# Seven-product pairs of an MLP: deeper look-ahead for weight loads, and convolutions issued one pair later

## The chip, the cores and the metric

The kernel runs on one core of a Trainium2 chip. The metric is device time in microseconds for one execution. Three runs of the kernel before the change took 1497.08 to 1503.07 us, with a median of 1500.95 us. The lines shown below come from one profiled execution.

The profile's engine names are PE (TensorE, matmul), PEld (TensorE's weight load), DVE (VectorE), ACT (ScalarE), POOL (GpSimd) and SP (SyncE). A "q" behind the name means the engine's queue of DMA issues and waits. L346 is line 346 of the kernel file.

## The reference

The kernel computes one layer of a hybrid backbone for 512 latent tokens and 128 context tokens, in float32. Three mixers run side by side, then comes a gated MLP. The change touches only the MLP:

```python
h2 = rms_norm(x, n2) * (1 + sc2) + sh2
u_val, u_gate = jnp.split(dw_conv(h2 @ w_up, f_conv), 2, axis=-1)
x = x + gt2 * ((jax.nn.silu(u_gate) * u_val) @ w_dn)
```

The model width is 1024 and the MLP's is 2816, so `w_up` is 1024 x 5632 and `w_dn` 2816 x 1024. `dw_conv` is a depthwise convolution of width 3 along the tokens.

## The kernel before, in words

All 640 tokens lie along the free dimension; features lie on the 128 partitions. A float32 product is made of three TensorE products of rounded parts: each operand is split into a high part (`wh`, a ScalarE cast, L149) and a low part (`wl`, a VectorE subtraction, L150).

The width of 2816 gives 22 feature tiles. Tiles 0 to 3 are computed plainly, as a value half (`uv`) and a gate half (`ug`). Tiles 4 to 21 are the 18 "pairs": `up_pair(f)` (L1672) computes value and gate together from seven products in place of eight, with sums of weights and sums of activations (a scheme of the Strassen kind). The tokens are cut into halves L and R of 320 columns. One product is 12 matmuls of 128 x 128 by 320 columns. They accumulate in three places: X and Y, the two banks of one large PSUM tile ("g", of which there are two), and Z in a small one ("s"). In the order of the program:

- product 1 into X and product 2 into Y, with the weights of entry 0;
- product 3 into Z and product 4 into X, entry 1;
- product 5 into Y and product 6 into Z, entry 2;
- product 7 into Y, entry 3.

Between them the partial sums are taken out into the tiles `u1` (value) and `u2` (gate): by ScalarE at L1689 (after product 1) and L1699 (4), and by VectorE at L1692 (2), L1696 (3), L1703 (5), L1706 (6) and L1710 (7). After product 7 come the convolutions of `u1` and `u2` (L1711 to L1713): for each one pass on ScalarE (L487) and four VectorE steps (L489). Then `gated` takes a silu on ScalarE (L1632), a multiplication on VectorE (L1633) and a split of the result (L379 on ScalarE, L380 on VectorE).

The pairs are grouped in blocks of 4, 4, 4, 3 and 3. While a block runs, each pair is followed by two or three products of the down projection of the block before it (`down`, L1718). Such a product is 18 or 24 matmuls into one "g" tile, which two or four VectorE steps empty into the residual tile `xa` (L1722). Since there are only two "g" tiles, pair and down products take turns in them.

Weights follow one plan, a list of entries in the order of use; `W(key)` hands out the next. It also issues the loads of the following two entries (`LOOK_L`) and the splits of the following one (`LOOK_S`). A pair has four entries, "st" 0 to 3, each a raw buffer of 128 x 1024. There are three raw buffers and two each for `wh` and `wl`. Entry 0 is one DMA on SyncE's queue (L248). Entries 1 and 2 have a second one that adds to the first in place, and runs on GpSimd's queue (L250), since it accumulates. The other sums of weights are made by VectorE: L258 (for entry 0, from the raw buffers of entries 0 and 1) and L260 (for entry 2, from those of 0 and 1). The weights of the down products have raw buffers and splits of their own (`rawd`, `whd`, `wld`, two each).

The order of the instructions in each engine's queue is not that of the program. A planner in the framework plays the program forward with costs of its own: an engine takes, among the instructions that are ready, the one with the earliest place in the program. Inside `tc.high_priority()` the place is counted as much earlier. That holds for loads, splits, sums of weights and for the lines that take the partial sums out; the convolutions, the gate and L1722 have plain priority. Once planned, the order in a queue is fixed.

Of the kernel before, what the change touches and what calls it, by code (L numbers as in the profile page):

```python
# [30 lines left out]
NF = DFF // P  # L31
GRP = 256
RAWB, WB = 3, 2
# [25 lines left out]
def hybrid_step(ctx: ExitStack, tc: tile.TileContext, a: dict, o: list):  # L59
# [18 lines left out]
    def gtile():  # L78
        return psg.tile([P, 1024], F32, tag="g", name=nm("g"))
# [7 lines left out]
    def body(ps):  # L87
        return ps[:, OFF:OFF + T]
# [44 lines left out]
    def w_load(pieces, kt, n, down=False):  # L133
        if down:
            raw = mlp["ep"].tile([P, 512], F32, tag="rawd", bufs=2, name=nm("rawd"))
        else:
            raw = ring.tile([P, 1024], F32, tag="raw", bufs=RAWB, name=nm("raw"))
        rv = raw[:, :kt * n].rearrange("p (k n) -> p k n", n=n)
        for src, c0, cn in pieces:
            SY.dma_start(out=rv[:, :, c0:c0 + cn], in_=src.rearrange("(k p) n -> p k n", p=P))  # L140
        return raw

    def w_split(raw, kt, n, down=False):
        if down:
            wh, wl = (mlp["ep"].tile([P, 512], F32R, tag=t, bufs=2, name=nm(t)) for t in ("whd", "wld"))
        else:
            wh, wl = (ring.tile([P, 1024], F32R, tag=t, bufs=WB, name=nm(t)) for t in ("wh", "wl"))
        m = kt * n
        S.copy(wh[:, :m], raw[:, :m])  # L149
        V.tensor_sub(wl[:, :m], raw[:, :m], wh[:, :m].bitcast(F32))  # L150
        vh = wh[:, :m].rearrange("p (k n) -> p k n", n=n)
        vl = wl[:, :m].rearrange("p (k n) -> p k n", n=n)
        return vh, vl

    plan = []
# [74 lines left out]

    pidx = {g[0]: i for i, g in enumerate(plan)}
    loaded, split = {}, {}
    LOOK_L, LOOK_S = 2, 1
    used = [0]


# [3 lines left out]
    def st_load(f, j):  # L240
        raw = st_raw[f, j] = ring.tile([P, 1024], F32, tag="raw", bufs=RAWB, name=nm("raw"))
        lo, hi = (raw[:, c:c + 512].rearrange("p (k n) -> p k n", n=P) for c in (0, 512))

        def part(r, kh):
            c0 = r * DFF + f * P
            return w_up[512 * kh:512 * kh + 512, c0:c0 + P].rearrange("(k p) n -> p k n", p=P)

        SY.dma_start(out=lo, in_=part(*((0, 0), (1, 0), (0, 0), (1, 1))[j]))  # L248
        if j in (1, 2):
            G.dma_start(out=lo, in_=part(1, 2 - j), accum_op=ALU.add)  # L250
        if j == 1:
            SY.dma_start(out=hi, in_=part(0, 1))
        return raw

    def st_sums(f, j):

        if j == 0:
            V.tensor_add(st_raw[f, 0][:, 512:], st_raw[f, 0][:, :512], st_raw[f, 1][:, :512])  # L258
        elif j == 2:
            V.tensor_add(st_raw[f, 2][:, 512:], st_raw[f, 0][:, 512:], st_raw[f, 1][:, 512:])  # L260

    def load_of(j):
        key, pieces, kt, n = plan[j]
        return st_load(*key[1:]) if key[0] == "st" else w_load(pieces, kt, n, key[0] == "wd")

    def split_of(j):
        key, pieces, kt, n = plan[j]
        if key[0] == "st":
            st_sums(*key[1:])
        return w_split(loaded[j], kt, n, key[0] == "wd")  # L270

    def W(key):
        i = pidx[key]
        assert i == used[0], (key, i, used[0])
        used[0] += 1
        with tc.high_priority() if i else nullcontext():
            for j in range(i, min(i + LOOK_L + 1, len(plan))):
                if j not in loaded:
                    loaded[j] = load_of(j)
            for j in range(i, min(i + LOOK_S + 1, len(plan))):  # L280
                if j not in split:
                    split[j] = split_of(j)
        return split[i]


# [47 lines left out]
    fcols = cp.tile([P, 3, 2 * NF], F32, name="fcols")  # L333
# [44 lines left out]
    def split_x(src, hi, lo):  # L378
        S.copy(hi, src)  # L379
        V.tensor_sub(lo, src, hi.bitcast(F32))  # L380
# [62 lines left out]
    n = NROW - R_N2  # L443
# [42 lines left out]
    def conv(y, src, w3):  # L486
        S.activation(out=y, in_=src, func=AF.Copy, scale=w3(1))  # L487
        for o0, o1, i0, t in ((1, TS, 0, 0), (0, TS - 1, 1, 2), (TS + 1, T, TS, 0), (TS, T - 1, TS + 1, 2)):
            V.scalar_tensor_tensor(out=y[:, o0:o1], in0=src[:, i0:i0 + o1 - o0], scalar=w3(t), in1=y[:, o0:o1],  # L489
                                   op0=ALU.mult, op1=ALU.add)  # L490
# [76 lines left out]
    for c in range(NCH):  # L567
# [3 lines left out]
        if c in (3, 4):  # L571
            n = c % 4 + 1
# [758 lines left out]
    for i, (sh, lo_, hi_) in enumerate(((8.0, 0.0, 1e9), (0.0, -1e9, 1e9), (0.0, -1e9, 16.0))):  # L1331

        st, t2 = mf[:, 2, :], mf[:, 3, :]
# [145 lines left out]
    for n, (before, steps, after) in enumerate(fill, -2):  # L1479

        if 1 <= n <= len(seq):
            t, j = seq[n - 1]
# [8 lines left out]
        if 0 <= n < len(seq):  # L1491
            t, j = seq[n]
# [29 lines left out]
    fslots = [ep.tile([P, T], F32, name=f"t{i}") for i in range(7)]  # L1522
# [4 lines left out]
    def rt(n=1):  # L1527
        return [slots.pop(0) for _ in range(n)]

    def ft():  # L1530
        return fslots.pop(0)
# [98 lines left out]
    def gated(f, uv, ug):  # L1630

        S.activation(out=ug, in_=ug, func=AF.Silu)  # L1632
        V.tensor_mul(uv, uv, ug)  # L1633
        ac[f] = rt(2)
        split_x(uv, *(t[:, :T] for t in ac[f]))
# [36 lines left out]
    def up_pair(f):  # L1672

        ps = gtile()
        X, Y, Z = ps[:, :HALF], ps[:, 512:512 + HALF], stile()[:, :HALF]

        def prod(out, w, kh, xx, start, stop):

            for k in range(4):
                for i, (ww, hl_) in enumerate(((w[0], 0), (w[0], 1), (w[1], 0))):  # L1680
                    PE.matmul(out=out, lhsT=ww[:, 4 * kh + k, :], rhs=xx(hl_, k), start=start and k == 0 and i == 0,  # L1681
                              stop=stop and k == 3 and i == 2, skip_group_check=True)

        hH2 = h2H, h2L
        u1, u2 = ft(), ft()
        w = W(("st", f, 0))
        prod(X, w, 0, lambda j, k: hH2[j][:, k, L], True, False)
        with tc.high_priority():
            S.copy(u2[:, L], X)  # L1689
        prod(Y, w, 1, lambda j, k: hs[k, 1][j][:, R], True, False)  # L1690
        with tc.high_priority():
            V.tensor_sub(u1[:, R], u2[:, L], Y)  # L1692
        w = W(("st", f, 1))
        prod(Z, w, 0, lambda j, k: hs[k, 0][j][:, L], True, False)
        with tc.high_priority():
            V.tensor_add(u2[:, R], u2[:, L], Z)  # L1696
        prod(X, w, 1, lambda j, k: hH2[j][:, 4 + k, L], False, True)
        with tc.high_priority():
            S.copy(u1[:, L], X)  # L1699
        w = W(("st", f, 2))  # L1700
        prod(Y, w, 0, lambda j, k: hs[k, 0][j][:, R], False, False)
        with tc.high_priority():
            V.tensor_sub(u2[:, R], Y, u2[:, R])  # L1703
        prod(Z, w, 1, lambda j, k: hH2[j][:, 4 + k, R], False, True)
        with tc.high_priority():
            V.tensor_add(u1[:, R], u1[:, R], Z)  # L1706
        w = W(("st", f, 3))
        prod(Y, w, 0, lambda j, k: hs[k, 1][j][:, L], False, True)
        with tc.high_priority():
            V.tensor_sub(u2[:, L], Y, u2[:, L])  # L1710
        ys = [ft() for _ in range(2)]  # L1711
        for y, u, f2 in zip(ys, (u1, u2), (f, NF + f)):
            conv(y, u, lambda tap, f2=f2: fcols[:, tap, f2:f2 + 1])  # L1713
        fslots.extend((u1, u2))
        gated(f, *ys)
        fslots.extend(ys)

    def down(b, nt):  # L1718
        ps = gtile()
        gemm_b(ps, W(("wd", b, nt)), lambda k: ac[fst[b] + k][0], lambda k: ac[fst[b] + k][1], FBLK[b])  # L1720
        for r, (c0, c1) in enumerate(((0, TS), (TS, T))):
            V.scalar_tensor_tensor(out=x1[nt][:, c0:c1], in0=body(ps)[:, c0:c1], scalar=modc[:, 40 + nt, r:r + 1],  # L1722
                                   in1=x1[nt][:, c0:c1], op0=ALU.mult, op1=ALU.add)
        if nt == 7:
            for k in range(FBLK[b]):
                slots.extend(ac.pop(fst[b] + k))
        if b == NB_F - 1:
            yt_ = ft()
            yt = chunks(yt_)
            tr_chunks(x1[nt], lambda c0, n, v: S.copy(yt[:, c0:c0 + n, :], v))  # L1730
            ns_ = slice(nt * P, (nt + 1) * P)
            SY.dma_start(out=y_s[0, :, ns_].rearrange("(c p) d -> p c d", p=P), in_=yt[:, 0:4, :])
            SY.dma_start(out=y_p[0, :, ns_], in_=yt[:, 4, :])
            fslots.append(yt_)
# [12 lines left out]
    for b in range(1, NB_F):  # L1747
        for i in range(FBLK[b]):
            up_pair(fst[b] + i)
            for nt in downs(b, i):  # L1750
                down(b - 1, nt)
    for nt in range(8):
        down(NB_F - 1, nt)

# [33 lines left out]
```

## Time and profile before

| | us |
|---|---|
| median of three runs | 1500.95 |
| the profiled execution | 1501.03 |
| its span on the core | 1498.4 |
| TensorE busy | 1351.9 |
| VectorE busy | 893.0 |
| ScalarE busy | 581.1 |
| GpSimd busy | 217.5 |
| first product 1 of a pair to the end of the last pair, about | 981 to 1458 |

In a row of the order of time, the first two numbers are the start and the duration in us, then come engine, line, operation, the tile written, the tiles read, and the count; brackets at the end give the idle time before it and what ended that. In a row of waits the numbers are the total in us, how often, and the longest. In a row of the chain of waits they are start and duration. A row over a stretch gives its ends, its length, the busy time of PE, PEld, DVE, ACT and POOL with counts, the granted TensorE clock, the DMA share and GB/s.

### The profile page before, as it was taken

The numbers are of one execution on the slowest core, as the hardware profiler recorded it, in microseconds if no ns is written. First come the engines' busy times: TensorE is split into PE (matmuls) and PEld (weight loads), VectorE is DVE, ScalarE is ACT, GpSimd is POOL, SyncE is SP. The second block draws the span as 40 slices with busy tenths as digits, with TensorE's granted clock in tenths as the row PEclk, the third lists the DMA queues.
The fourth block names the chain that finished last, engine by engine and source line by source line (L and its number), as shares of the span: only waits on it lengthen the run. The fifth ranks groups of instructions, "written<-read, shape, count | busy, mean of one in ns | idle before, by whom it ended". The sixth has DMA issues, their size and how long they took to land.

```text
span 1498.4 us, 27051 instructions
## 1 busy us (share of the span) xinstructions
PE 1351.9 (90%) x10985; PEld 1263.0 (84%) x10985; DVE 893.0 (60%) x1863; ACT 581.1 (39%) x1080; POOL 217.5 (15%) x224
## 2 busy tenths in 40 slices
PE   6998999989798999999999899888888787887888
PEld 4898999989687989999988899878777787877887
DVE  4775876776887533433342545985665756566554
ACT  4552235224855322333332354743333333332233
POOL 1011022021343110121200311000101010010000
PEclk9999999999999999999999999999999999999899
DMA  9423421331111533443454442233434334343223
GB/s 277 135 66 91 107 53 36 78 75 37 29 37 48 101 92 102 120 108 97 128 158 122 126 129 72 50 85 81 91 82 98 92 90 98 81 90 89 65 59 108
DMA packets 228079, 137.97 MB, mean 92 GB/s; under 512 B 22037, under 2 KB 221491, under 8 KB 227955
## 3 DMA queue, kind: packets, MB, share of 16 engines
q1 hardware_dynamic: 208563, 126.48, 31.1%
q0 software_dynamic: 19008, 9.44, 5.2%
q8 instruction: 86, 1.41, 0.4%
q10 hardware_dynamic: 384, 0.33, 0.1%
q14 instruction: 38, 0.31, 0.1%
HBM read 129.67 MB, written 6.55 MB: 91 GB/s over the span
## 4 chain that ended last, share of the span: by engine, by line
PE 45%; DVE 17%; DMA 10%; ACT 4%; issue 4%; POOL 3%; SPq 0%; ACTq 0%; POOLq 0%; DVEq 0%
PE g L346 30%; DMA raw<-in_w_up_dram 9%; PE g L1681 6%; DVE t L489 5%; DVE wl L150 4%; ACT wh L149 1%; DVE wld L150 1%; PE s L394 1%; PE s L594 1%; DVE xa L1722 1%; PE g L367 1%; PE s L1420 1%; PE s L1408 1%; PE m L1370 1%; DMA XT<-Xd 1%
## 5 line engine op out<-in xcount | busy, mean ns | idle before, releaser
L149 ACT CAST wh<-raw 128x1024 fp32r<-128x1024 f32 (+1 forms) x176 | 164.8, 945 | 381.8 <-PE g L346 168.6
L150 DVE TENSOR_TENSOR wl<-raw,wh 128x1024 fp32r<-128x1024 f32 (+1 forms) x176 | 192.8, 1098 | 168.5 <-ACT wh L149 158.9
L346 PE MATMUL g<-hH,wh 128*128 128x320 f32 x768 | 186.1, 321 | 3.0 <-DVE xb L702 1.5
L346 PE MATMUL g<-r,whd 128*128 128x320 f32 x704 | 149.7, 334 | 42.6 <-DVE t L1710 31.7
L346 PE MATMUL g<-hL,wh 128*128 128x320 f32 x768 | 183.7, 317 | 0.6 <-DVE hL L442 0.6
L346 PE MATMUL g<-hH,wl 128*128 128x320 f32 x768 | 182.5, 316 | 0.0
L346 PEld LDWEIGHTS g<-r,whd 128*128 128x128 f32 x704 | 121.8, 207 | 48.8 <-DVE t L1710 36.1
L346 PEld LDWEIGHTS g<-hH,wh 128*128 128x128 f32 x768 | 128.8, 191 | 11.3 <-issue 3.9
L346 PEld LDWEIGHTS g<-hL,wh 128*128 128x128 f32 x768 | 130.2, 190 | 3.4 <-issue 1.8
L346 PEld LDWEIGHTS g<-hH,wl 128*128 128x128 f32 x768 | 131.0, 191 | 2.2 <-issue 1.9
L250 POOL DMA_DIRECT2D raw<-in_w_up_dram x36 | 46.4, 1290 | 461.7 <-DMA raw<-in_w_up_dram 383.3
L1681 PE MATMUL g<-r,wh 128*128 128x320 f32 x432 | 101.3, 321 | 0.1
L367 PE MATMUL g<-wh,hH 128*128 128x256 f32 x320 | 94.4, 295 | 3.4 <-DVE xb L702 3.4
L367 PE MATMUL g<-wl,hH 128*128 128x256 f32 x320 | 94.1, 294 | 0.0
L367 PE MATMUL g<-wh,hL 128*128 128x256 f32 x320 | 93.7, 293 | 0.0
L346 PE MATMUL g<-r,wld 128*128 128x320 f32 x352 | 87.9, 327 | 0.0
L1681 PE MATMUL g<-h2H,wh 128*128 128x320 f32 x144 | 51.3, 356 | 40.4 <-DVE xa L1722 38.9
L489 DVE SCALAR_TENSOR_TENSOR t<-t,fcols,t 128x511 f32<-128x511 f32 (+1 forms) x156 | 78.4, 544 | 1.0 <-ACT t L487 1.0
L1681 PEld LDWEIGHTS g<-r,wh 128*128 128x128 f32 x432 | 72.4, 192 | 6.4 <-DVE t L1703 3.3
L346 PE MATMUL g<-oz,wh 128*128 128x320 f32 x384 | 73.8, 314 | 1.3 <-DVE xb L1281 1.2
L1681 PEld LDWEIGHTS g<-h2H,wh 128*128 128x128 f32 x144 | 29.8, 207 | 45.8 <-issue 42.2
L367 PEld LDWEIGHTS g<-wh,hH 128*128 128x128 f32 x320 | 62.8, 196 | 5.2 <-DVE xb L702 3.6
(592 smaller groups left out, 2974.0 us busy)
## 6 DMA issues: line engine op xcount, KB each, us to landing
raw<-in_w_in_dram SPq DMA_DIRECT2D x64, 512.0 KB
raw<-in_w_up_dram SPq DMA_DIRECT2D x90, 256.0 KB
wada<-in_w_ada_dram SPq DMA_DIRECT2D x32, 512.0 KB
raw<-in_w_up_dram POOLq DMA_DIRECT2D x36, 256.0 KB, 4.8
wat<-in_w_ada_dram SPq DMA_DIRECT2D x16, 512.0 KB
rawd<-in_w_down_dram SPq DMA_DIRECT2D x32, 256.0 KB
raw<-in_w_branch_dram SPq DMA_DIRECT2D x24, 256.0 KB
raw<-in_w_out_dram SPq DMA_DIRECT2D x8, 512.0 KB
```

The costliest lines, as they stand in the source:

```text
L149: S.copy(wh[:, :m], raw[:, :m])
L150: V.tensor_sub(wl[:, :m], raw[:, :m], wh[:, :m].bitcast(F32))
L250: G.dma_start(out=lo, in_=part(1, 2 - j), accum_op=ALU.add)
L346: PE.matmul(out=ps[:, OFF + c0:OFF + c1], lhsT=ww[:, k, :], rhs=xx(k)[:, c0:c1], start=(k == 0 and i == 0), stop=(k == kt - 1 and i == 2))
L367: PE.matmul(out=ps[b][:, o:o + GRP], lhsT=xx[:, 4 * kh + k, cs], rhs=ww[:, k, :], start=(kh == 0 and c % 2 == 0 and k == 0 and i == 0), st ...
L394: PE.matmul(out=pa[32 * g:32 * g + 32, :w], lhsT=csil[:, k, :], rhs=t[g], start=start, stop=stop)
L489: V.scalar_tensor_tensor(out=y[:, o0:o1], in0=src[:, i0:i0 + o1 - o0], scalar=w3(t), in1=y[:, o0:o1], op0=ALU.mult, op1=ALU.add)
L594: PE.transpose(pt[:, i * P:(i + 1) * P], src[:, (c0 + i) * P:(c0 + i + 1) * P], ident)
L1370: PE.matmul(out=ps[:, 0:256], lhsT=qT_[t][b, qs], rhs=kT_[t][b, :TS].rearrange("p (r k) -> p r k", k=64)[:, :, CST[j]:CST[j] + 32], start= ...
L1408: PE.transpose(pt[:, i * P:(i + 1) * P], Pt[:, i * P:(i + 1) * P], ident)
L1420: PE.matmul(out=po[64 * e:64 * e + 64, 0:P], lhsT=v[:, h * HD:(h + 1) * HD], rhs=PT[:, i * P:(i + 1) * P], start=(i == 0), stop=(i == len( ...
L1681: PE.matmul(out=out, lhsT=ww[:, 4 * kh + k, :], rhs=xx(hl_, k), start=start and k == 0 and i == 0, stop=stop and k == 3 and i == 2, skip_g ...
```

## The change

Two things are changed. First, in the entries "uv", "ug", "st" and "wd", `W` also issues loads up to six entries ahead (`LOOK_F`), as far as `may_load` allows: the last user of the buffer must have been issued already. Second, `up_pair` no longer issues the convolutions and the gate of its own pair at its end. It puts them into a list `later` as a generator with three parts (convolution of `u2`, convolution of `u1`, gate). `some()` runs one part, and is called at four places in the next pair: after products 4 and 5, and twice after product 6. What is left after the last pair runs behind its down products. The convolution of `u2` now comes ahead of that of `u1`.

```diff
-    LOOK_L, LOOK_S = 2, 1
+    LOOK_L, LOOK_S, LOOK_F = 2, 1, 6
...
+    def may_load(j):
+
+        down = plan[j][0][0] == "wd"
+        same = [i for i in range(j) if (plan[i][0][0] == "wd") == down]
+        n = 2 if down else RAWB
+        if len(same) < n:
+            return down
+        i = same[-n]
+        if i not in split:
+            return False
+        key = plan[i][0]
+        return key[0] != "st" or key[2] > 1 or pidx["st", key[1], 2] in split
...
+            if key[0] in ("uv", "ug", "st", "wd"):
+                for j in range(i + LOOK_L + 1, min(i + LOOK_F + 1, len(plan))):
+                    if j not in loaded:
+                        if not may_load(j):
+                            break
+                        loaded[j] = load_of(j)
...
             S.copy(u1[:, L], X)
+        some()
         w = W(("st", f, 2))
         prod(Y, w, 0, lambda j, k: hs[k, 0][j][:, R], False, False)
         with tc.high_priority():
             V.tensor_sub(u2[:, R], Y, u2[:, R])
+        some()
         prod(Z, w, 1, lambda j, k: hH2[j][:, 4 + k, R], False, True)
         with tc.high_priority():
             V.tensor_add(u1[:, R], u1[:, R], Z)
+        some()
+        some()
         w = W(("st", f, 3))
...
-        ys = [ft() for _ in range(2)]
-        for y, u, f2 in zip(ys, (u1, u2), (f, NF + f)):
-            conv(y, u, lambda tap, f2=f2: fcols[:, tap, f2:f2 + 1])
-        fslots.extend((u1, u2))
-        gated(f, *ys)
+        later.append(finish(f, u1, u2))
+
+    def finish(f, u1, u2):
+
+        ys = []
+        for u, f2 in ((u2, NF + f), (u1, f)):
+            ys.append(ft())
+            conv(ys[-1], u, lambda tap, f2=f2: fcols[:, tap, f2:f2 + 1])
+            fslots.append(u)
+            yield
+        gated(f, ys[1], ys[0])
         fslots.extend(ys)
+        yield
+
+    later = []
+
+    def some():
+        if later:
+            if next(later[0], 0) == 0:
+                later.pop(0)
...
             for nt in downs(b, i):
                 down(b - 1, nt)
+    while later:
+        some()
     for nt in range(8):
         down(NB_F - 1, nt)
```

## The prediction

> **What bounds the kernel now.** I read the busy shares first, then the stage of the pairs alone, then who waited there, then the chain of waits, and last the instructions of one pair in order of time. Engine shares, and the queue of the accumulating loads:
>
> ```profile
> PE 1351.9 (90%) x10985; PEld 1263.0 (84%) x10985; DVE 893.0 (60%) x1863; ACT 581.1 (39%) x1080; POOL 217.5 (15%) x224
> ...
> raw<-in_w_up_dram POOLq DMA_DIRECT2D x36, 256.0 KB, 4.8
> ```
>
> The 90% are an average. The change touches the 18 pairs. Their stretch (columns: us, then PE, PEld, DVE, ACT, POOL busy), the copies of product 1, and one pair in the middle:
>
> ```profile
> 981.20:1458.00 476.80, 396.04 (x2377) 374.82 (x2378) 291.44 (x490) 153.83 (x218) 43.66 (x34) 0.94 0.38 85
> ```
> ```profile
> L1689 ACT COPY t<-g x18: 425/426/429, 983.3 to 1447.7; 128x320 f32<-128x320 f32 x18
> ```
> ```profile
> 1237.41:1264.26 26.85, 22.10 (x132) 20.93 (x132) 16.17 (x28) 8.60 (x12) 2.56 (x2) 0.94 0.40 88
> ```
>
> So TensorE idles 80.8 us in this stage, the turns are (1447.7 - 983.3)/17 = 27.3 us long on average, and the middle one lasts 26.85 us with TensorE busy for 22.10 and VectorE for 16.17. Neither fills it: it must be a loop of latencies. What TensorE waited for between 981 and 1458 us (us in total, times, longest):
>
> ```profile
> PE g L1681 <- DVE xa L1722: 38.9, 14, 3.2
> PE g L346 <- DVE t L1710: 31.7, 17, 2.7
> PE g L346 <- DVE xa L1722: 8.9, 3, 3.2
> ```
>
> Both waits are for VectorE to empty a PSUM tile. The chain of waits gives the loads between two pairs:
>
> ```profile
> 1254.49 1.24 DVE wl L150
> 1255.74 3.15 DMA raw<-in_w_up_dram
> 1259.46 4.77 DMA raw<-in_w_up_dram
> ```
>
> The low part of entry 2 (its "wl") frees a raw buffer, the next pair's entry 1 is loaded into it, GpSimd's accumulating load adds to it, and VectorE's sum L258 takes it at 1259.46 + 4.77 = 1264.23. VectorE from one L258 to the next wl of entry 2:
>
> ```profile
> 1237.41 0.69 DVE L258 TENSOR_TENSOR raw<-raw,raw 128x512 f32<-128x512 f32 x1 [3.92 <-DMA raw<-in_w_up_dram]
> 1238.03 0.48 DVE L1710 TENSOR_TENSOR t<-g,t 128x320 f32<-128x320 f32 x1
> 1238.42 0.68 DVE L260 TENSOR_TENSOR raw<-raw,raw 128x512 f32<-128x512 f32 x1
> 1239.02 0.74 DVE L489 SCALAR_TENSOR_TENSOR t<-t,fcols,t 128x511 f32<-128x511 f32 x1
> 1239.68 1.22 DVE L150 TENSOR_TENSOR wl<-raw,wh 128x1024 fp32r<-128x1024 f32 x1
> 1240.82 0.69 DVE L150 TENSOR_TENSOR wld<-rawd,whd 128x512 fp32r<-128x512 f32 x1
> 1241.43 1.22 DVE L150 TENSOR_TENSOR wl<-raw,wh 128x1024 fp32r<-128x1024 f32 x1
> 1242.56 1.66 DVE L489 SCALAR_TENSOR_TENSOR t<-t,fcols,t 128x511 f32<-128x511 f32 x3
> 1244.15 0.68 DVE L150 TENSOR_TENSOR wld<-rawd,whd 128x512 fp32r<-128x512 f32 x1
> 1244.75 1.26 DVE L489 SCALAR_TENSOR_TENSOR t<-t,fcols,t 128x127 f32<-128x127 f32 x3
> 1245.93 0.74 DVE L1722 SCALAR_TENSOR_TENSOR xa<-g,modc,xa 128x512 f32<-128x512 f32 x1
> 1246.60 0.34 DVE L489 SCALAR_TENSOR_TENSOR t<-t,fcols,t 128x127 f32<-128x127 f32 x1
> 1246.85 1.00 DVE L1722 SCALAR_TENSOR_TENSOR xa<-g,modc,xa 128x128 f32<-128x128 f32 x2
> 1247.80 0.83 DVE L1633 TENSOR_TENSOR t<-t,t 128x640 f32<-128x640 f32 x1
> 1248.54 0.35 DVE L1722 SCALAR_TENSOR_TENSOR xa<-g,modc,xa 128x128 f32<-128x128 f32 x1
> 1249.42 0.82 DVE L380 TENSOR_TENSOR r<-t,r 128x640 fp32r<-128x640 f32 x1 [0.53 <-ACT r L379]
> 1250.61 0.49 DVE L1696 TENSOR_TENSOR t<-t,s 128x320 f32<-128x320 f32 x1 [0.37 <-ACT t L1689]
> 1253.56 0.49 DVE L1692 TENSOR_TENSOR t<-t,g 128x320 f32<-128x320 f32 x1 [2.46 <-PE g L1681]
> 1254.49 1.23 DVE L150 TENSOR_TENSOR wl<-raw,wh 128x1024 fp32r<-128x1024 f32 x1 [0.44 <-ACT wh L149]
> ```
>
> This is the loop. VectorE waits 3.92 us for the load, then works 13 us without a pause, and the tile that the next pair needs ("xa", from the first down product) is emptied only behind seven of the eight convolution steps. TensorE meanwhile:
>
> ```profile
> 1238.56 0.86 PE L346 MATMUL g<-r,whd 128*128 128x320 f32 x4 [1.74 <-DVE t L1710]
> ...
> 1242.20 0.46 PE L1681 MATMUL s<-r,wh 128*128 128x320 f32 x2
> ...
> 1247.34 0.39 PE L1681 MATMUL g<-h2H,wh 128*128 128x320 f32 x1 [2.91 <-DVE xa L1722]
> ...
> 1248.58 0.47 PE L1681 MATMUL g<-h2L,wh 128*128 128x320 f32 x1
> 1248.85 0.47 PE L1681 MATMUL g<-h2H,wl 128*128 128x320 f32 x1
> ```
>
> The 24 matmuls of the second down product take 1242.20 - 1238.56 = 3.64 us, 0.15 us each. Then product 3 of the next pair runs, ahead of its product 1, so the order in a queue is not the program's. After the 2.91 us pause, matmuls start 0.27 us apart for some 3 us.
>
> The turn is therefore 17.08 us (L258 at 1237.41 to wl at 1254.49) + 9.76 (wl to the next L258 at 1264.25) = 26.84. Of the 17.08, 0.53 + 0.37 + 2.46 + 0.44 = 3.80 are pauses and 13.28 work.
>
> **The change part by part. Loads up to six entries ahead.** Instructions and bytes stay the same; only the place in the program moves. There are still three raw buffers for four entries a pair, and a load can't start before its buffer is free. In the turn above the load leaves at 1255.74, when the wl that frees its buffer ends (1254.49 + 1.23 = 1255.72). It already leaves as early as it can, so the part costs and gives nothing. Its bounds: at worst a load of w_up stands ahead of one of w_down in SyncE's queue, whose data are used a whole turn later; at best it takes 0.02 us from a turn. I take 0. GpSimd's accumulating loads keep their order.
>
> The load term of 4.77 us is the longest step of the loop. The Trainium skill ("DMA: Bandwidth & Descriptors", Anatomy of one DMA — SWDGE path) fits such a transfer by about 2.0 us plus bytes over 436e3; for 256 KB that is 2.6 us, and the sum below would come 2.2 us per turn, 37 us in all, lower, at about 1407. The 36 transfers here have a median of 4.8, and that stands.
>
> **The convolutions and the gate.** Nothing is added or removed: per pair two ScalarE passes, eight VectorE steps (0.74 + 1.66 + 1.26 + 0.34 = 4.0 us), silu, L1633 and the split L380 (0.83 + 0.82). They move behind the down products and products 4 to 6 of the next pair, so they lose their precedence over "xa". They don't necessarily run there: their inputs are ready as soon as L1710 is done, and queues take what is ready, as the early product 3 shows. So I take that they still run in this burst, but after "xa".
>
> First effect, on TensorE. Take the seven steps ahead of "xa" (3.66 us) away and it is emptied by about 1243.5. Product 3 ends near 1244.4 (1247.34 - 2.91), and product 1 starts there: the 2.91 us pause goes, with most of the slow matmuls behind it. Products 1 and 2 with the six down matmuls between them are 30 matmuls, 4.5 us, so product 2 ends at 1248.9, where today L1692 waits for it until 1253.56.
>
> Second effect, on the loop. L1696 and L1692 no longer find VectorE waiting for TensorE: 0.37 and 2.46 go, and these two, now ready, fill the 0.53 in front of L380. The wait for ScalarE's cast (0.44) stays. What is late next is VectorE itself: 13.28 us of work in its queue between L258 and wl. The new turn is 13.28 + 0.44 + 9.76 = 23.48 us, 3.36 less than 26.84. TensorE needs 132 x 0.15 = 19.8 and isn't the bound; its wait for L1710 stays.
>
> The sum: 17 turns x 3.36 = 57 us. The last pair's convolutions now come behind the "xa" of its down products (0.74 + 1.00 + 0.35 = 2.1 us for two), and the last products read their result; between 0 and 2.1 I take 1. The profiled execution took 1501.03 (span 1498.4 and 2.6 around it), the median of the runs is 1500.95: 1501 - 57 + 1 = 1445.
>
> Bounds of the turn: if the convolution and gate leave the stretch between L258 and wl altogether, 13.28 - 5.65 + 0.44 + 9.76 = 17.8, less than TensorE's 19.8, so 20; if all pauses stay, 26.84. I take the value nearest to the rows as they stand, the full work without TensorE's pauses.
>
> **The rivals.** A: the written place holds, and a good part of the 5.65 us falls behind wl, where VectorE now idles before L258. For it: these steps have the lowest precedence, and wl comes earlier than before. Against: they are ready some 10 us before wl. With L1633 and L380 alone behind it the turn is 21.8 and the time 1501 - 17 x 5.0 = 1416; with all, 20 and 1501 - 17 x 6.85 = 1385.
>
> B: nothing. "xa" goes ahead, but another wait takes the place: product 1 also needs the wl of entry 0 (1239.68 to 1240.9), and L1710 holds the second down product. For it: VectorE's work per turn is the same. Against: both are done 3 us before 1244.4. The turn stays 26.8: 1501. A half-way case, with 1 us per turn gained, gives 1484.
>
> C, slower: the sum L258 moves ahead of L1703 in VectorE's queue, since wl and its load come earlier against product 5. VectorE takes its queue in order (today L1710 starts only when L258 has run, and TensorE waits 1.74 us for it), so L1703 would wait for the load, and product 7 behind it. After L258: 0.6 + 0.5 for L1703, 12 matmuls 1.8, 13 of the down product 2.0, 24 more 3.6, product 3 1.8: product 1 at 10.3 us after L258 (9.93 today), 1.4 later still since TensorE's pause of some 4 us makes 12 matmuls slow (12 x 0.12). Then 4.5 for products 1 and 2, 1.1 for the cast, 9.76 of loading: 27.1. It is a loss once product 1 comes over 11.5 us after L258; with half a microsecond more, 27.4 and 1510. Against: L1703 comes well ahead of L258 now, 1264.25 - 1259.14 = 5.1 us:
>
> ```profile
> 1259.14 0.49 DVE L1703 TENSOR_TENSOR t<-g,t 128x320 f32<-128x320 f32 x1 [1.78 <-PE g L1681]
> ```
>
> The Trainium skill ("TensorE: Matmul & The Clock Gate", Part 1) has the array at half rate after an idle window of about 3.4 us, until 3.4 us of work have passed; by it C's pause costs 1.7 us and not 1.4, and its turn is 27.4 at once. Here a pause of 2.91 was enough for slow matmuls, so the trace is harsher than that page.
>
> **How the numbers follow.** Forecast (turn 22.3 to 25, 1425 to 1475) 0.50; A 0.24; the half-way case 0.09; B 0.08; C 0.09. What a measurement can tell here is about 0.5%, 7.5 us. Faster by more: 0.50 + 0.24 + 0.08 of the half-way case = 0.82; same 0.09; slower 0.09. The range from 1392 to 1497 takes in nearly all of A and the half-way case and leaves out B, C and the end of A, about 0.2. The forecast's own range is 1425 to 1475.
>
> **What would show it.** The turn between copies of product 1 falls to 23.5; the 38.9 us of waits for "xa" nearly vanish, the 31.7 for L1710 stay; in VectorE's queue "xa" stands ahead of most of L489, and wl follows L1692 without a pause for TensorE; loads leave within 0.1 us of the wl that frees their buffer, as before. It is wrong if L489 runs behind wl (A), if product 1 still waits (B), or if L258 precedes L1703 (C).

## The result, and the profile after

Four runs of each kernel gave a median of 1424.15 us after (1420.27 to 1429.12) against 1499.62 before (1497.08 to 1503.07): a ratio of 0.9497 with a 95% interval of 0.9461 to 0.9533. The profiled execution's span fell from 1498.4 to 1422.9 us. The forecast was 1445; the time is 21 us under it, inside the wide range of 1392 to 1497 and 1 us below the forecast's own range of 1425 to 1475.

The edit shifts line numbers. In the rows of after, L1708 is the copy of product 1 (before L1689), L1711 and L1715 are the steps L1692 and L1696, L1723 and L1727 are L1703 and L1706, L1733 is L1710, L1759 empties "xa" (L1722), L508 is the convolution (L489), L1651 and L1652 are silu and L1633, L399 is the gate's split (L380). L150, L248, L250, L258 and L260 stay.

First the page of after, its row of busy shares and that of the accumulating loads:

```profile
PE 1330.2 (93%) x10985; PEld 1243.6 (87%) x10985; DVE 891.1 (63%) x1863; ACT 578.9 (41%) x1080; POOL 217.7 (15%) x224
...
raw<-in_w_up_dram POOLq DMA_DIRECT2D x36, 256.0 KB, 4.7
```

The work is the same, instruction for instruction. Then the stage of the pairs by itself (columns as before: us, then PE, PEld, DVE, ACT, POOL busy, granted clock), and the copies of product 1:

```profile
985.00:1382.00 397.00, 369.05 (x2362) 349.40 (x2362) 286.75 (x487) 149.98 (x216) 43.66 (x34) 0.99 0.46 103
```
```profile
L1708 ACT COPY t<-g x18: 405/414/428, 985.0 to 1372.2; 128x320 f32<-128x320 f32 x18
```

The mean turn is (1372.2 - 985.0)/17 = 22.77 us, before 27.32: 17 x 4.55 = 77 us, which is the whole gain; the stage starts 1.7 us later, and what follows the last copy is as long as it was (50.7 us). In this stage TensorE's idle time fell from 80.8 to 28.0 us, and the granted clock is 0.99 in place of 0.94. The row of after begins and ends a little inside the stage and leaves out 15 of the matmuls that the row of before counts. From 982.90 to 1382.40 us, with 2377 on record in both, TensorE is busy for 371.45 us, 24.6 less than before for the same matmuls. The 53 us of idle time and these 24.6 make up the 77. What TensorE still waits for there (us in total, times, longest):

```profile
PE g L1700 <- DVE xa L1759: 10.8, 13, 1.4
PE g L365 <- DVE t L1733: 8.7, 14, 2.8
PE g L1700 <- ACT t L1708: 3.7, 11, 0.5
```

VectorE in one turn in the middle, from one L258 to the next, in order of time:

```profile
1198.58 0.69 DVE L258 TENSOR_TENSOR raw<-raw,raw 128x512 f32<-128x512 f32 x1 [3.40 <-DMA raw<-in_w_up_dram]
1199.18 0.75 DVE L508 SCALAR_TENSOR_TENSOR t<-t,fcols,t 128x511 f32<-128x511 f32 x1
1199.84 0.48 DVE L1733 TENSOR_TENSOR t<-g,t 128x320 f32<-128x320 f32 x1
...
1203.12 0.74 DVE L1759 SCALAR_TENSOR_TENSOR xa<-g,modc,xa 128x512 f32<-128x512 f32 x1
...
1204.38 0.34 DVE L1759 SCALAR_TENSOR_TENSOR xa<-g,modc,xa 128x128 f32<-128x128 f32 x1
1204.64 1.93 DVE L508 SCALAR_TENSOR_TENSOR t<-t,fcols,t 128x511 f32<-128x511 f32 x4
1206.48 0.74 DVE L1759 SCALAR_TENSOR_TENSOR xa<-g,modc,xa 128x512 f32<-128x512 f32 x1
...
1208.00 1.39 DVE L508 SCALAR_TENSOR_TENSOR t<-t,fcols,t 128x511 f32<-128x511 f32 x3
1209.50 0.83 DVE L1652 TENSOR_TENSOR t<-t,t 128x640 f32<-128x640 f32 x1
1210.24 0.48 DVE L1711 TENSOR_TENSOR t<-t,g 128x320 f32<-128x320 f32 x1
1210.77 1.23 DVE L150 TENSOR_TENSOR wl<-raw,wh 128x1024 fp32r<-128x1024 f32 x1
1211.91 0.48 DVE L1715 TENSOR_TENSOR t<-t,s 128x320 f32<-128x320 f32 x1
1212.31 0.82 DVE L399 TENSOR_TENSOR r<-t,r 128x640 fp32r<-128x640 f32 x1
...
1220.42 0.69 DVE L258 TENSOR_TENSOR raw<-raw,raw 128x512 f32<-128x512 f32 x1 [3.45 <-DMA raw<-in_w_up_dram]
```

Three things are to be seen. The first "xa" now stands ahead of seven of the eight convolution steps. From L258 to the wl of entry 2 VectorE no longer pauses for another engine: 12.19 us, and no pause is marked in it (before 17.08, with 3.80 us of pauses). And L1715 and the split L399 have moved behind that wl. From the wl to the next L258 the turn is as before, 9.65 us (9.76); the chain of waits shows the two loads that fill it, the first 0.02 us behind the wl's end (1210.77 + 1.23 = 1212.00):

```profile
1212.02 3.09 DMA raw<-in_w_up_dram
...
1215.67 4.72 DMA raw<-in_w_up_dram
```

(As what released the first one the chain names a TensorE matmul that was running just then. Its end is modelled; the buffer is read by the cast and the wl alone, and the 0.02 us behind the wl is also the distance of before, 1255.72 to 1255.74.)

TensorE at product 1 and product 2 of the same turn, and ScalarE beside it:

```profile
1204.86 0.38 PE L1700 MATMUL g<-h2H,wh 128*128 128x320 f32 x1 [0.68 <-DVE xa L1759]
1205.09 0.31 PE L1700 MATMUL g<-h2L,wh 128*128 128x320 f32 x1
1205.23 0.31 PE L1700 MATMUL g<-h2H,wl 128*128 128x320 f32 x1
...
1207.76 0.56 PE L1700 MATMUL g<-r,wh 128*128 128x320 f32 x2 [0.30 <-ACT t L1708]
```
```profile
1206.65 0.74 ACT L1651 ACTIVATE t<-t 128x640 f32<-128x640 f32 x1 [2.11 <-DVE t L508]
1207.30 0.41 ACT L1708 COPY t<-g 128x320 f32<-128x320 f32 x1
1209.68 1.05 ACT L149 CAST wh<-raw 128x1024 fp32r<-128x1024 f32 x1 [1.98 <-PE g L1700]
```

The pause before product 1 is 0.68 us where it was 2.91. Behind the first one the matmuls start 0.15 us apart and stay so; before, six of them did, and those from 1248.31 to 1251.5 us were 0.27 apart. ScalarE has become the second way round the loop: the copy of product 1 stands behind silu in its queue, product 2 waits 0.30 us for the copy, and the cast that the wl needs starts when product 2 is done. It ends at 1209.68 + 1.05 = 1210.73, and L1711 ends at 1210.24 + 0.48 = 1210.72: the two ways to the wl now tie.

### The profile page after: what moved, and what is told of

Its sections match the earlier page's. It is cut to its first block, busy times and chain, and to the rows that moved or that the text cites. A ratio compares the mean times of both kernels' runs of the same rounds, so it can differ in the third digit from the quotient of the medians.

```text
span 1422.9 us, 27064 instructions
## 1 busy us (share of the span) xinstructions
PE 1330.2 (93%) x10985; PEld 1243.6 (87%) x10985; DVE 891.1 (63%) x1863; ACT 578.9 (41%) x1080; POOL 217.7 (15%) x224
## 4 chain that ended last, share of the span: by engine, by line
PE 50%; DVE 17%; DMA 10%; issue 5%; ACT 3%; POOL 3%; ACTq 0%; SPq 0%; POOLq 0%; DVEq 0%
PE g L365 30%; DMA raw<-in_w_up_dram 9%; PE g L1700 5%; DVE t L508 4%; DVE wl L150 3%; PE g L386 2%; PE s L1700 2%; DVE xa L1759 1%; PE s L613 1%; PE s L413 1%; PE s L1439 1%; DVE wld L150 1%; PE s L1427 1%; ACT wh L149 1%; POOL ssn L335 1%
## 5 line engine op out<-in xcount | busy, mean ns | idle before, releaser
L150 DVE TENSOR_TENSOR wl<-raw,wh 128x1024 fp32r<-128x1024 f32 (+1 forms) x176 | 192.3, 1101 | 153.3 <-ACT wh L149 143.3
L365 PE MATMUL g<-r,whd 128*128 128x320 f32 x704 | 139.2, 317 | 10.8 <-DVE t L1733 8.7
L365 PEld LDWEIGHTS g<-hH,wh 128*128 128x128 f32 x768 | 129.1, 191 | 11.5 <-issue 3.9
L365 PEld LDWEIGHTS g<-r,whd 128*128 128x128 f32 x704 | 111.8, 191 | 16.7 <-DVE t L1733 12.9
L250 POOL DMA_DIRECT2D raw<-in_w_up_dram x36 | 46.4, 1290 | 386.9 <-DMA raw<-in_w_up_dram 294.2
L365 PE MATMUL g<-r,wld 128*128 128x320 f32 x352 | 81.0, 311 | 0.0
L508 DVE SCALAR_TENSOR_TENSOR t<-t,fcols,t 128x511 f32<-128x511 f32 (+1 forms) x156 | 78.5, 543 | 3.4 <-ACT t L506 2.9
L1700 PE MATMUL g<-r,wl 128*128 128x320 f32 x216 | 66.7, 309 | 0.0
L386 PEld LDWEIGHTS g<-wl,hH 128*128 128x128 f32 x320 | 63.7, 199 | 0.0
```

The lines of the kernel that those rows point to most:

```text
L365: PE.matmul(out=ps[:, OFF + c0:OFF + c1], lhsT=ww[:, k, :], rhs=xx(k)[:, c0:c1], start=(k == 0 and i == 0), stop=(k == kt - 1 and i == 2))
L386: PE.matmul(out=ps[b][:, o:o + GRP], lhsT=xx[:, 4 * kh + k, cs], rhs=ww[:, k, :], start=(kh == 0 and c % 2 == 0 and k == 0 and i == 0), st ...
```

## The experiments

The theory: the time of a turn is a loop (load of entry 1, L258, VectorE's queue up to the wl of entry 2, load again), and the gain comes wholly from "xa" going ahead of the convolutions in VectorE's queue. Rivals: the loads' look-ahead brings part of it; the place between the next pair's products brings it; the total of VectorE's work, or TensorE, is the bound and not the loop. The runs, with medians in us, the ratio to the kernel before on the same chip, and the mean turn from the copies of product 1:

| run | this / before | ratio [95%] | mean turn |
|---|---|---|---|
| e1_look_only | 1502.62 / 1497.27 | 1.0037 [1.0016, 1.0059] | 27.04 |
| e2_later_only | 1425.34 / 1497.27 | 0.9515 [0.9492, 0.9539] | 22.65 |
| e3_after_own_downs | 1425.41 / 1497.27 | 0.9517 [0.9497, 0.9537] | 22.66 |
| e4_xa_high | 1408.30 / 1497.65 | 0.9408 [0.9392, 0.9423] | 21.88 |
| e5_raw4 | 1419.00 / 1497.65 | 0.9478 [0.9447, 0.9509] | 22.21 |
| e6_no_acc1 | 1396.43 / 1497.65 | 0.9335 [0.9313, 0.9358] | 21.12 |
| e7_gate_high | 1435.14 / 1497.27 | 0.9580 [0.9552, 0.9608] | 23.31 |
| e8_sum_twice | 1448.99 / 1497.65 | 0.9683 [0.9653, 0.9713] | 24.12 |
| e9_split_twice | 1425.60 / 1500.71 | 0.9510 [0.9467, 0.9552] | 22.66 |
| e10_split_first | 1472.17 / 1500.71 | 0.9816 [0.9766, 0.9866] | 25.18 |
| c1_both | 1427.40 / 1500.71 | 0.9518 [0.9471, 0.9565] | 22.81 |
| c2_sum_behind | 1420.73 / 1498.72 | 0.9486 [0.9458, 0.9513] | 22.41 |

**The two parts by themselves.** e1 is the kernel before with the look-ahead alone (LOOK_F, may_load and the loop that uses them); e2 is the change without it:

```
-    LOOK_L, LOOK_S, LOOK_F = 2, 1, 6
+    LOOK_L, LOOK_S, LOOK_F = 2, 1, 2
```

> The look-ahead of six entries alone; convolutions and gate as before. Theory O (order): loads already leave when the wl that frees their buffer ends, so nothing changes: turn 26.8 us, time 1500, within 4. Rival L (look-ahead): the loads leave earlier and shorten the loop; then at least a third of the 75 us gained comes from here, 1475 or less.

> Convolutions and gate moved, look-ahead back at two entries. Theory O: all of the gain, turn 21.8 us, time 1424, within 5. Rival L: what look-ahead brings is lost, 1445 or more.

The look-ahead alone brings nothing, if anything 0.4% the wrong way. In its trace VectorE's pause for TensorE ahead of the wl is the one of before to the hundredth:

```profile
1229.42 0.49 DVE L1711 TENSOR_TENSOR t<-t,g 128x320 f32<-128x320 f32 x1 [2.46 <-PE g L1700]
1230.36 1.23 DVE L150 TENSOR_TENSOR wl<-raw,wh 128x1024 fp32r<-128x1024 f32 x1 [0.45 <-ACT wh L149]
```

The moved convolutions alone bring all of the gain: 0.9515 against 0.9497, with overlapping intervals.

**Does it matter where they are placed?** e3 runs the same parts straight behind the pair's own down products, none between the next pair's products:

```
             for nt in downs(b, i):
                 down(b - 1, nt)
+            while later:
+                some()
```
(the calls of some() between the products are gone, and so is the loop behind the last pair)

> The changed kernel, but the three parts of a pair are issued straight behind its own down products, none between the products of the next pair. Theory O: what counts is that xa comes ahead of them in VectorE's queue, which holds here too: 1424, within 8. Rival P (place): the place between the products lets VectorE fill its pauses; without it the gate is back ahead of wl, the turn is 23 us or more and the time 1445 or more.

It gives the same time and the same order in VectorE's queue. What counts is that the steps of "xa" stand ahead of the convolutions in the program, not how far behind them these stand.

**Precedence alone.** e4 is the kernel before, nothing moved, with the two steps of L1722 raised in priority:

```
-        for r, (c0, c1) in enumerate(((0, TS), (TS, T))):
-            V.scalar_tensor_tensor(...)
+        with tc.high_priority():
+            for r, (c0, c1) in enumerate(((0, TS), (TS, T))):
+                V.scalar_tensor_tensor(...)
```

> The kernel before, with only the two steps that empty a down product (xa) put at high priority; convolutions stay at the end of their pair, look-ahead at two. Theory O: the precedence of xa over L489 is the cause, so most of the gain comes: 1424 to 1440. Rival P (place): the convolutions have to move, so it stays near 1497, 1475 or more.

It came out better than expected, and beats the changed kernel by 16 us (13 by the ratios, 0.9408 against 0.9497, whose intervals lie apart). So the precedence of "xa" by itself gives the whole gain and more, and the change isn't the best use of it. The swapped order of the two convolutions isn't needed either, as e4 keeps the old one. Its stage of the pairs, and VectorE and ScalarE in one turn (here L1723 is "xa", the other lines are those of before):

```profile
983.00:1365.00 382.00, 364.39 (x2351) 344.57 (x2350) 284.47 (x487) 150.10 (x215) 43.65 (x34) 1.00 0.48 107
```
```profile
1192.04 0.69 DVE L258 TENSOR_TENSOR raw<-raw,raw 128x512 f32<-128x512 f32 x1 [1.96 <-DMA raw<-in_w_up_dram]
...
1203.67 1.22 DVE L150 TENSOR_TENSOR wl<-raw,wh 128x1024 fp32r<-128x1024 f32 x1
...
1210.58 0.48 DVE L1710 TENSOR_TENSOR t<-g,t 128x320 f32<-128x320 f32 x1
1213.00 0.69 DVE L258 TENSOR_TENSOR raw<-raw,raw 128x512 f32<-128x512 f32 x1 [1.93 <-DMA raw<-in_w_up_dram]
```
```profile
1198.49 0.43 ACT L1689 COPY t<-g 128x320 f32<-128x320 f32 x1 [1.70 <-PE g L1681]
1201.76 0.74 ACT L1632 ACTIVATE t<-t 128x640 f32<-128x640 f32 x1 [2.84 <-DVE t L489]
```

L258 to wl is 11.63 us (12.19 after the change) and wl to L258 9.33 (9.65): 0.88 us per turn, 17 turns, 15 of the 17 us by which the spans differ (1405.7 against 1422.9). Two differences in the order are to be seen. L1710 and a convolution step run in VectorE's pause ahead of L258, where the change has them behind it; and the copy of product 1 runs ahead of silu on ScalarE, so that the cast is ready earlier. How much the second carries, no run here separates; c2 below tries the first.

**Both together, and the order forced.** c1 adds e4's edit to the change. c2 adds to the change an order in VectorE's queue, L258 behind the step that takes out product 7 (L1733), as in e4:

```
+            add = V.tensor_add(st_raw[f, 0][:, 512:], ...)
+            if out7:
+                tc.add_manual_dep(add.ins, out7[-1].ins.name, ..., reason="sum behind product 7")
...
+            out7.append(V.tensor_sub(u2[:, L], Y, u2[:, L]))
```

> The changed kernel and, with it, xa at high priority (the edit of e4). Theory O with the loop: moving the convolutions adds nothing to what the precedence of xa gives, 1405 to 1412; the floor is TensorE's 132 matmuls, turn 20, 1393. Rival P: the two gains add up, 1385 or less.

> The changed kernel with one order forced on VectorE's queue: the sum L258 behind the step that takes out product 7 (L1710 of the kernel before, L1733 of the changed one), as the plan of e4 has it and the change has not. Theory O with the loop: that step's slot of 0.40 us leaves the stretch from L258 to wl, and with it up to two convolution steps (0.66 each) that can run in VectorE's pause: turn 20.5 to 21.4 us, 1402 to 1418. If the order of these two makes nothing of the difference between e4 and the change: 1425.

Both missed: neither is told from the change alone. In c1 silu still precedes the copy of product 1, and L258 to wl is 12.18 us as in the change:

```profile
1212.12 0.74 ACT L1651 ACTIVATE t<-t 128x640 f32<-128x640 f32 x1 [2.11 <-DVE t L508]
1212.76 0.41 ACT L1708 COPY t<-g 128x320 f32<-128x320 f32 x1
```

In c2 the order did move (here L260 is the sum and L1738 the step of product 7), but the turn stayed at 1221.52 - 1199.66 = 21.86:

```profile
1199.66 0.69 DVE L260 TENSOR_TENSOR raw<-raw,raw 128x512 f32<-128x512 f32 x1 [0.90 <-DMA raw<-in_w_up_dram]
...
1210.26 0.83 DVE L1657 TENSOR_TENSOR t<-t,t 128x640 f32<-128x640 f32 x1 [0.21 <-ACT t L1656]
...
1211.72 1.23 DVE L150 TENSOR_TENSOR wl<-raw,wh 128x1024 fp32r<-128x1024 f32 x1 [0.23 <-ACT wh L149]
...
1219.74 0.49 DVE L1738 TENSOR_TENSOR t<-g,t 128x320 f32<-128x320 f32 x1
1221.52 0.69 DVE L260 TENSOR_TENSOR raw<-raw,raw 128x512 f32<-128x512 f32 x1 [1.29 <-DMA raw<-in_w_up_dram]
```

L1738 and a convolution step (0.40 and 0.66 us of the queue) left the stretch from the sum to the wl, but the counterpart of L1715 (0.40) came into it with two pauses for ScalarE, 0.21 and 0.23: 12.06 us where the change has 12.19. From 1195 to 1225 us the chain of waits of c2 runs almost only through TensorE:

```profile
by line: PE g L370 41.8%; PE g L1705 39.9%; PE s L1705 14.0%; DVE wl L150 3.8%; issue 1.1%; DVEq L150 0.2%
```

The way over the load, 12.06 us and 9.80 from the wl to the next sum, closes at the same 21.86, so this run doesn't tell which of the two sets the turn.

**Is the load on the loop, and is VectorE's total off it?** e6 is the change without entry 1's accumulating load; e9 is the change with the low part of the split L399 computed twice, behind the wl:

```
-        if j in (1, 2):
+        if j == 2:
             G.dma_start(out=lo, in_=part(1, 2 - j), accum_op=ALU.add)
```
```
+        V.tensor_sub(ac[f][1][:, :T], uv, ac[f][0][:, :T].bitcast(F32))
```

> The changed kernel without the accumulating load of entry 1 (that part of the weights is left out). Theory O with the loop: 4.8 us fall out of the loop, TensorE becomes the bound: turn 19.8 to 20.6, 1390 to 1405. If the load isn't on the loop: 1424.

> The changed kernel with the low part of the gate's split (L399) made twice. It stands behind wl in VectorE's queue, where VectorE later waits 3.4 us for the load. Theory O with the loop: off the loop, 1421 to 1428, though VectorE works 0.74 us more per turn. If VectorE's total work is the bound: 17 x 0.74 = 13 us more, 1437.

Both times came as expected. Without the load of 4.7 us the turn falls to 20.27 in the middle (its mean, 21.12, stays above the expected 19.8 to 20.6). TensorE is busy for 19.93 of these 20.27 us, so it is close to being the bound. L258 still waits for a DMA, but 1.22 us and not 3.4:

```profile
1203.52 0.69 DVE L258 TENSOR_TENSOR raw<-raw,raw 128x512 f32<-128x512 f32 x1 [1.22 <-DMA raw<-in_w_up_dram]
...
1223.79 0.69 DVE L258 TENSOR_TENSOR raw<-raw,raw 128x512 f32<-128x512 f32 x1 [1.22 <-DMA raw<-in_w_up_dram]
```

The turn fell by 1.6 us and not by the load's 4.7: from the wl to L258 it is 4.40 us in place of 9.65, but from L258 to the wl 15.87 in place of 12.19, since L258, ready so early, now has L1723, L1727 and more behind it in the queue. The second split, 0.8 us of VectorE's work per pair in the stretch with pauses between the wl and the next L258, costs nothing that can be measured. So VectorE's total is not the bound. Whether its work between L258 and the wl is, the next runs ask.

**What one step more or less inside the loop costs.** e8 makes the sum L258 twice, e7 raises the gate's priority, e10 (from e3) orders the wl of entry 2 behind the gate's split:

```
+            V.tensor_add(st_raw[f, 0][:, 512:], st_raw[f, 0][:, :512], st_raw[f, 1][:, :512])
```
```
-        gated(f, ys[1], ys[0])
+        with tc.high_priority():
+            gated(f, ys[1], ys[0])
```
```
+        if key[0] == "st" and key[2] == 2 and key[1] > FBLK[0]:
+            tc.add_manual_dep(low[0].ins, gsplit[0].ins.name, ..., reason="split before wl")
```

> The changed kernel with the sum L258 made twice; it lies between the load's landing and wl. Theory O with the loop: each turn grows by its slot of 0.61 us, 17 x 0.61 = 10 us: 1432 to 1438. If VectorE's work there isn't on the loop: 1424 to 1427.

> The changed kernel with the gate (silu, multiplication, split) at high priority, so that its split runs ahead of wl again. Theory O with the loop from L258 over wl and the two loads back to L258: each turn grows by the split's 0.74 us slot and up to 0.5 us of waiting for ScalarE's cast, 13 to 21 us in all: 1437 to 1445. If VectorE's queue between L258 and wl is not on the loop: 1424.

> The kernel of e3 (parts issued behind their own down products) with an order forced on VectorE's queue: wl of entry 2 behind the split of the gate of the pair before. Theory O with the loop, and the term missed in the prediction: the split's slot of 0.74 us, and up to 0.5 of waiting for ScalarE's cast, come back into the stretch from L258 to wl: turn 22.6 to 23.1, 13 to 21 us over 1425: 1438 to 1446. If that place doesn't matter: 1425.

All three are slower than the change. e8 and e10 put work into the loop, and cost more than the step that they add: both missed, e8 by 11 us and e10 by 26. In e8 L258 to wl went from 12.19 to 13.72 us in most turns for a step of 0.6, because the order around it changed as well: the counterpart of L1715 (0.40) came back ahead of the wl, with some 0.4 us of pauses for ScalarE. In two turns it was 14.86, as a "wld" waited for ScalarE besides (first row). In e10 it went to 14.68 in the middle: the split, its wait for the cast of its high part, and the counterpart of L1715, which had moved ahead of the wl and waited 1.70 us for ScalarE:

```profile
1220.09 0.69 DVE L150 TENSOR_TENSOR wld<-rawd,whd 128x512 fp32r<-128x512 f32 x1 [1.04 <-ACT whd L149]
```
```profile
1216.33 0.49 DVE L1722 TENSOR_TENSOR t<-t,s 128x320 f32<-128x320 f32 x1 [1.70 <-ACT t L1715]
...
1220.38 0.83 DVE L1661 TENSOR_TENSOR r<-t,r 128x640 fp32r<-128x640 f32 x1 [0.80 <-ACT r L1660]
```

e7, at 1435, came 2 us short of its expected 1437 to 1445, but its split still stood behind the wl, so it doesn't test the split's place. The sign of these runs supports the loop; their sizes price a whole new order, not one step.

**Does a fourth raw buffer open the loop?** e5 is e2 with one raw buffer for each of the four entries from the second pair on (six scratch tiles in place of seven make room):

```
+        if f > FBLK[0]:
+            if j not in raw4:
+                raw4[j] = mlp["e2"].tile(...) if j == 3 else ring.tile(...)
+            raw = st_raw[f, j] = raw4[j]
...
-    fslots = [ep.tile([P, T], F32, name=f"t{i}") for i in range(7)]
+    fslots = [ep.tile([P, T], F32, name=f"t{i}") for i in range(6)]
```

> Convolutions moved as in the change, look-ahead at two, and from the second pair on four raw buffers, one for each entry (and six in place of seven scratch tiles, to make the room). Theory O with the loop: the load of entry 1 no longer waits for the wl of entry 2, the loop is open, and TensorE's 132 matmuls with small waits are the bound: turn 19.8 to 20.6 us, 20 to 35 us less than the changed kernel: 1390 to 1405. If the loop doesn't run through that buffer: 1425.

It missed by 14 us. The buffer that entry 1's load needs now comes free with entry 1's own wl, and the loop closed over that one (here L263 is the sum):

```profile
1217.40 1.22 DVE L150 TENSOR_TENSOR wl<-raw,wh 128x1024 fp32r<-128x1024 f32 x1
...
1227.07 0.69 DVE L263 TENSOR_TENSOR raw<-raw,raw 128x512 f32<-128x512 f32 x1 [2.45 <-DMA raw<-in_w_up_dram]
...
1239.24 1.22 DVE L150 TENSOR_TENSOR wl<-raw,wh 128x1024 fp32r<-128x1024 f32 x1
```

From that wl to the sum are 9.67 us, from the sum to the next such wl 12.17: 21.84 again. The planned order also put the sum later, behind seven of the eight convolution steps.

## Why the prediction was right, and where it was off

**The look-ahead at 0** was right (e1), for the reason given: the loads leave within 0.02 us of the wl that frees their buffer in both kernels.

**Precedence, not place** was right (e2, e3, e4): "xa" goes ahead of the convolutions, which run in the same burst behind it.

**TensorE's pauses** went as worked out: the 2.91 us ahead of product 1 became 0.68, the waits of 0.37, 2.46 and 0.53 us in VectorE's queue are gone. Product 1 waits 10.8 us for "xa" in the stage, where it waited 38.9.

**The term that was mis-sized**, and by which the time left the forecast's own range, is "13.28 us of work in its queue between L258 and wl", with the 0.44 for the cast: 13.72 was predicted, 12.19 measured. The split (0.74 us of the queue) and L1696 (0.40) moved behind the wl, and of the 0.44 for the cast 0.05 is left, as VectorE comes to the wl at the moment when the cast ends. 0.74 + 0.40 + 0.39 = 1.53 us per turn, 26 us in 17 turns. This is rival A by half: it had the split and L1633 behind the wl (1416). The prediction named the reason (the lowest precedence, and a wl that comes earlier) and set it too low; that L1696 could go there as well it had not seen. (VectorE doesn't work "13 us without a pause" behind L258, as the prediction says: it is 11.5 us, from 1237.41 to 1248.89. The 13.28 are the work in the whole 17.08, and the sum used them rightly.) The rows of before gave a hint: the split's input came 0.53 us late there, so a wl that is ready earlier can pass it.

**The loading part**, 9.76 predicted and 9.65 measured, held. For its longest step the Trainium skill ("DMA: Bandwidth & Descriptors", Anatomy of one DMA — SWDGE (gpsimd) path) would give an estimate of 2.6 us for 256 KB. The accumulating loads measure 4.7 after and 4.8 before, so keeping the measured value was right.

**One turn carried over to all 17.** The middle turn fell by 5.00 us, the mean by 4.55, which is 8 us in 17 turns. Over half of that comes from three turns of the kernel before that took only 25.1 to 25.2 us from L258 to L258 and fell by 3.4 to 3.7: in them the granted clock stayed at 1.00 during products 1 and 2. The rest is spread over the other turns. By chance this hid part of the miss: 26 for the queue, 2 for the loads and 1 for the tail, less 8, are the 21 us between 1445 and 1424.

**"The wait for L1710 stays"** was wrong: 31.7 us became 8.7. TensorE does the same matmuls in a turn that is 5 us shorter, so it comes to the second down product 1.5 us behind L258 where it came 0.6 us ahead of it, and finds the step nearly done (a wait of 0.26 us in the middle turn, before 1.74). **The tail** of 1 us was not there (50.7 us behind the last copy in both). **Rivals B and C** didn't occur: product 1 starts early, and L258 stays behind L1723.

## What to carry to other kernels

Where an engine takes its queue in order, look for what stands ahead of the step that empties the PSUM tile another engine waits for: to raise that one step can be worth more than to move the work around it, and is two lines. Where a buffer's release bounds a load, issuing the load earlier in the program brings nothing; count the work between the landing and the step that frees the buffer, and expect the loop to close over the next such step when one is opened. Where a planner sets the order, one more step or one forced pair can change the whole queue: read the new order before the time is put down to the step.

## What the runs showed of the hardware that was not expected

What slow matmuls behind a pause cost in all. The waits of product 1 for "xa" fell by 28 us (38.9 to 10.8), and TensorE's busy time for the same matmuls fell by 24.6 beside it, nearly as much again. In e4, whose longest such wait is 1.3 us, 2362 matmuls take 366.30 us, where the change takes 369.05. The prediction had these 0.27 us steps in its turn, but gave them no price of their own.

The granted clock shows where this comes from. In the stage of the pairs it is either 1.00 or 0.50, and each stretch at 0.50 is 3.41 us long: 17 of them before, 2 after, none in e4. An estimate from these, 15 x 3.41 x 0.5 = 25.6 us, agrees with the 24.6. The middle turn of before, in steps of that length:

```profile
1241.43:1244.84 3.41, 2.96 (x19) 2.44 (x17) 3.41 (x7) 0.63 (x2) 0.00 (x0) 1.00 0.64 184
1244.85:1248.26 3.41, 0.92 (x6) 0.95 (x7) 3.41 (x8) 0.74 (x1) 0.00 (x0) 1.00 0.43 123
1248.26:1251.67 3.41, 3.41 (x15) 3.41 (x14) 1.94 (x4) 1.16 (x2) 0.00 (x0) 0.50 0.02 5
```

The half clock begins 0.92 us behind the pause, at the end of a step in which TensorE was busy for 0.92 of 3.41 us. So it was with all 17: TensorE was busy for 15 to 49% of the 3.41 us before. Three steps of before at 46 to 50% were not followed by half clock, so where the border lies is not settled.

The Trainium skill ("TensorE: Matmul & The Clock Gate", Part 1) puts half rate behind an idle window of about 3.4 us. The stretches here have that length, but the step ahead of them was not idle throughout: the waits of before were at most 3.2 us long by the view of waits, and half clock followed one of 2.91 us. Behind the pause of 0.68 us there was none.
